# A causal convolution with matrices as taps: twelve outputs from four half-size convolutions in place of eight from three

## The chip, the cores and the metric

The kernel runs on one core of one Trainium2 chip. The core has a matrix engine (TensorE, "PE" in the profile), a vector engine (VectorE, "DVE"), a scalar engine (ScalarE, "ACT"), GpSimd ("POOL", which here only issues transfers that cast) and SyncE ("SP", which here issues stores and transposing transfers). Transfers run on 16 DMA engines. The metric is device time in microseconds (us) for one execution, as the median of several.

## The reference

```python
B, S, D, K = 8, 4096, 512, 8          # x: (8, 4096, 512) float32, kernel: (8, 512, 512) float32
out = np.zeros_like(x)
for k in range(K):
    shifted = x if k == 0 else np.concatenate([np.zeros((B, k, D)), x[:, :-k, :]], axis=1)
    out += np.matmul(shifted, kernel[k])
```

Each output row is the sum of eight products, `out[t] = x[t] W0 + x[t-1] W1 + ... + x[t-7] W7`, with 512 x 512 matrices as taps: a convolution in t whose coefficients are matrices. Done directly, one row costs eight row-by-matrix products.

## The kernel before

The 32768 rows are cut into 128 runs of 256 consecutive rows. One run belongs to each of the 128 partitions, and the kernel goes through the runs in step: "row t" below means row t of all 128 runs. Row t, transposed, is a tile of 128 partitions by 512 (four blocks of 128 channels by 128 runs), and serves as the stationary operand. A *product* is one such row times one 512 x 512 matrix, in bfloat16 with float32 sums in PSUM: four matmuls of 128x128 by 128x512.

```python
def product(bank, comp, w, start):
    for c in range(DC):                                   # DC = 4
        nc.tensor.matmul(bank, lhsT=comp[:, c * P:(c + 1) * P], rhs=w[:, c, :],
                         start=start and c == 0, stop=c == DC - 1, ...)
```

The kernel saves products in the manner of Karatsuba. Eight outputs with eight taps are made from three *half-size convolutions* of four outputs and four taps each: one with the low half of the taps, one with the high half, one with their difference (`LO`, `HI`, `MID`). Their inputs are sums of rows (`D4[t] = x[t-4] + x[t]`, and so on), made by VectorE. The same step is used twice more inside each, so that one half-size convolution, called a *node*, takes 9 products in place of 16. An iteration of the loop makes eight rows with three nodes, 27 products; there are 32 iterations.

A node uses three pairs of PSUM banks in turn for its four outputs (`p[0]` and `p[1]`, two outputs each) and a fourth pair `q` for what its parts share:

```python
def node_a1(k):                    # first product of a node; ScalarE copies it to the other bank
    product(n.q[:, 1], n.s[1][1], W[a, MID, HI], True)
    nc.scalar.copy(out=n.q[:, 0], in_=n.q[:, 1])
def node_a0(n):   product(n.q[:, 0], n.s[1][0], W[n.a, MID, LO], False)
def node_u(n):    product(n.q[:, 1], n.s[0], W[n.a, MID, MID], False)
def node_seed(n, b_):              # ScalarE starts a bank with +q or -q
    n.p[b_] = pair((2 * n.k + b_) % 3)
    ... nc.scalar.copy / nc.scalar.mul(-1.0)  (out=n.p[b_][:, 1], in_=n.q[:, 1])
def node_dts(n):  nc.scalar.copy(out=n.dts, in_=n.q[:, 0])
def node_v(n, b_): product(n.p[b_][:, 1], n.s[2][b_], W[n.a, b_, MID], False)
def node_d(n, b_):                 # VectorE starts the other bank
    tt(p[:, 0], n.dts, p[:, 1], SUB)            # or scalar_tensor_tensor for b_ == HI
def node_l(n, b_, j):              # one of the four last products
    product(n.p[b_][:, j], n.s[3][2 * b_ + j], W[n.a, b_, j], False)
def node_e(n, b_):                 # eviction of two outputs
    if n.a == MID:  nc.scalar.copy(out=ms[b_], in_=p)
    else:           tt(y, p, ms[b_], ADD if n.a == LO else SUB); store(n.i, n.a, b_, y)
```

In the loop the products of one node are interleaved with the start of the next:

```python
for k, (i, a) in enumerate(order):               # from k == 6 on
    if a == MID and more: transpose_x(i + 1, 0)
    node_l(cur, 0, LO); node_l(cur, 0, HI)
    node_a0(nxt); node_u(nxt)
    node_l(cur, 1, LO); node_e(cur, 0)
    node_seed(nxt, 0); node_seed(nxt, 1); node_dts(nxt)
    ...                                          # VectorE makes sums for later nodes
    node_v(nxt, 0); node_d(nxt, 0); node_v(nxt, 1); node_d(nxt, 1)
    ...
    node_l(cur, 1, HI); node_a1(k + 2); node_e(cur, 1)
    ...                                          # transpose_x(i + 1, 1), load_x(i + 2, ...)
```

Rows of x come in pieces of four rows: GpSimd issues a load that casts float32 in DRAM to bfloat16 in SBUF (`xin`, two buffers), and SyncE issues a transfer that transposes `xin` into `XT`, also in SBUF. The first nodes are the set-up: the weights are loaded there and their differences made, the first rows are transposed on TensorE, node 0 makes its four outputs directly with 16 products, and five nodes finish the first 16 rows. On TensorE 24 matmuls of zeros (`fill`) stand in the set-up's gaps.

Of the kernel before, what the change touches and what calls it, by code (L numbers as in the profile page):

```python
# [8 lines left out]

LO, HI, MID = 0, 1, 2


@with_exitstack
def kernel(
# [13 lines left out]
    NIT = RUN // K  # L37
    assert K == 8 and D == 512 and S % RUN == 0 and RUN % K == 0
# [13 lines left out]
    xpool = ctx.enter_context(tc.tile_pool(name="x", bufs=2))  # L52

    ctx.enter_context(tc.manual_schedule())

    W = {}
    for a in (LO, HI, MID):
        for b_ in (LO, HI, MID):
            for c_ in (LO, HI, MID):
                W[a, b_, c_] = wpool.tile([P, DC, D], bf, name=f"w{a}{b_}{c_}")  # L60

    XT = spool.tile([P, K, D], bf, name="XT")
    D4 = spool.tile([P, K, D], bf, name="D4")
    D42 = spool.tile([P, K, D], bf, name="D42")
    D421 = spool.tile([P, K, D], bf, name="D421")
    D41 = spool.tile([P, 4, D], bf, name="D41")
    D2 = spool.tile([P, 5, D], bf, name="D2")
    D21 = spool.tile([P, 4, D], bf, name="D21")
    D1 = spool.tile([P, 2, D], bf, name="D1")

    F21 = spool.tile([P, 4, D], bf, name="F21")
    F0 = spool.tile([P, D], bf, name="F0")
    A1 = spool.tile([P, 2, D], bf, name="A1")
# [4 lines left out]

    def load(out, src):
        nc.gpsimd.dma_start(out=out, in_=src)  # L80

    xin = {}

    def load_x(i, h):
        xin[i, h] = xpool.tile([P, 4, D], bf, name="xin")
        load(xin[i, h], xr[:, K * i + 4 * h:K * i + 4 * h + 4, :])

    def transpose_x(i, h):
        nc.sync.dma_start_transpose(
            out=XT[:, 4 * h:4 * h + 4, :].rearrange("p j (c m) -> p (j c) m", m=P),  # L90
            in_=xin[i, h].rearrange("p j d -> p (j d)"))


    def pairs(z):
        return z.rearrange("p (a b) d -> p a (b d)", b=2)

    def prep_m():

        tt(D1[:, 0:2], XT[:, 7::-7], XT[:, 0:2], ADD)
        tt(pairs(D2[:, 1:5]), pairs(XT)[:, 3::-3], pairs(XT)[:, 0:2], ADD)  # L100

    def prep_d27():
        tt(D2[:, 0], XT[:, 5], XT[:, 7], ADD)

    def prep_d21():
        tt(D21[:, 0:4], D2[:, 0:4], D2[:, 1:5], ADD)

    def prep_d4(h):
        a, b = (XT[:, 4:8], XT[:, 0:4]) if h == LO else (XT[:, 0:4], XT[:, 4:8])
        tt(D4[:, 4 * h:4 * h + 4], a, b, ADD)  # L110

    def prep_d41(h):
        if h == LO:
            tt(D41[:, 0:2], D4[:, 7::-7], D4[:, 0:2], ADD)
        else:
            tt(D41[:, 2:4], D4[:, 3:5], D4[:, 4:6], ADD)

    def prep_d42(h):
        if h == LO:
            tt(pairs(D42)[:, 0:2], pairs(D4)[:, 3::-3], pairs(D4)[:, 0:2], ADD)  # L120
        else:
            tt(D42[:, 4:8], D4[:, 2:6], D4[:, 4:8], ADD)

    def prep_d421(h):
        if h == LO:
            tt(D421[:, 0:4:2], D42[:, 7:0:-6], D42[:, 0:4:2], ADD)
            tt(D421[:, 1:4:2], D42[:, 0:4:2], D42[:, 1:4:2], ADD)
        else:
            tt(D421[:, 4:8], D42[:, 3:7], D42[:, 4:8], ADD)

    ppool = ctx.enter_context(tc.tile_pool(name="p", bufs=1, space=PSUM))

    def pair(k):
        return ppool.tile([P, 2, D], f32, name=f"pp{k}")

    H, HF = XT, D421.bitcast(f32).rearrange("p (t b) d -> p t (b d)", b=2)
    nc.sync.dma_start(out=HF, in_=xr[:, RUN - 4:RUN, :])
    load_x(0, 0)
    zero = spool.tile([P, D], bf, name="zero")
    nc.vector.memset(zero, 0.0)  # L145
    U1 = zero
# [5 lines left out]
    def mid(level, u, v):  # L152

        if level == 0:
            return W[MID, u, v], W[HI, u, v], W[LO, u, v]
        if level == 1:
            return W[u, MID, v], W[u, HI, v], W[u, LO, v]
        return W[u, v, MID], W[u, v, LO], W[u, v, HI]

    def mid_dve(*which):  # L160
        o, u, v = mid(*which)
        tt(o, u, v, SUB)


    def mid_neg(u, v):
        nc.scalar.mul(out=W[MID, u, v], in_=W[LO, u, v], mul=-1.0)

    def mid_acc(u, v):
        nc.gpsimd.dma_start(out=W[MID, u, v], in_=W[HI, u, v], accum_op=ADD)

    load_w(4)
    load(H[:, 1:4], xr[:, RUN - 7:RUN - 4, :])
    ident = spool.tile([P, P], bf, name="ident")
    make_identity(nc, ident)
    bank = {}

    def fill(pw):

        for h in range(2):
            nc.tensor.matmul(pw[:, h], lhsT=zero[:, 0:P], rhs=zero, start=True, stop=True)  # L180

# [7 lines left out]

    for k in range(6):  # L190
        fill(pair(k % 4))
    XF = D42


    def product(bank, comp, w, start):
        for c in range(DC):
            nc.tensor.matmul(bank, lhsT=comp[:, c * P:(c + 1) * P], rhs=w[:, c, :],  # L197
                             start=start and c == 0, stop=c == DC - 1,
                             skip_group_check=True)

    mpool = ctx.enter_context(tc.tile_pool(name="m", bufs=2))
    cpool = ctx.enter_context(tc.tile_pool(name="c", bufs=2))
    fpool = ctx.enter_context(tc.tile_pool(name="f", bufs=2))
    ypool = ctx.enter_context(tc.tile_pool(name="y", bufs=4))

    class Node:
        pass

    def streams(i, a):

        if a == MID and i == 0:
            return (F0, [D1[:, 0], D1[:, 1]], [D2[:, 1], D2[:, 3]],
                    [F21[:, j] for j in range(4)])
        if (i, a) == (1, MID):
            return (U1, [A1[:, 0], A1[:, 1]], [D21[:, 0], D21[:, 2]],
                    [F21[:, j] for j in range(4)])
        if a == MID:
            return (XT[:, 0], [D1[:, 0], D1[:, 1]], [D2[:, 1], D2[:, 3]],
                    [D21[:, j] for j in range(4)])
        o = 4 * a  # L220
        if (i, a) == (1, LO):
            return (T4[:, 0], [D41[:, 0], D41[:, 1]], [T42[:, 0], T42[:, 2]],
                    [D421[:, j] for j in range(4)])
        if (i, a) == (1, HI):
            return (D4[:, 4], [D41[:, 2], D41[:, 3]], [D42[:, 4], D42[:, 6]],
                    [D421[:, j] for j in range(4)])
        return (D4[:, o], [D41[:, 2 * a], D41[:, 2 * a + 1]], [D42[:, o], D42[:, o + 2]],
                [D421[:, o + j] for j in range(4)])

    def node_a1(k):
        n = Node()
        nodes.append(n)
        n.k, (n.i, n.a) = k, order[k]
        a = n.a  # L240
        n.s = streams(n.i, a)
        n.q = pair(3)
        product(n.q[:, 1], n.s[1][1], W[a, MID, HI], True)
        nc.scalar.copy(out=n.q[:, 0], in_=n.q[:, 1])  # L244
        n.p = {}

    def node_a0(n):
        product(n.q[:, 0], n.s[1][0], W[n.a, MID, LO], False)

    def node_u(n):  # L250
        product(n.q[:, 1], n.s[0], W[n.a, MID, MID], False)

    def node_seed(n, b_):
        n.p[b_] = pair((2 * n.k + b_) % 3)
        if b_ == LO:
            nc.scalar.copy(out=n.p[b_][:, 1], in_=n.q[:, 1])  # L256
        else:
            nc.scalar.mul(out=n.p[b_][:, 1], in_=n.q[:, 1], mul=-1.0)  # L258

    def node_dts(n):  # L260
        n.dts = cpool.tile([P, D], f32, name="dts")
        nc.scalar.copy(out=n.dts, in_=n.q[:, 0])  # L262

    def node_v(n, b_):
        product(n.p[b_][:, 1], n.s[2][b_], W[n.a, b_, MID], False)

    def node_d(n, b_):
        p = n.p[b_]
        if b_ == LO:
            tt(p[:, 0], n.dts, p[:, 1], SUB)  # L270
        else:
            nc.vector.scalar_tensor_tensor(out=p[:, 0], in0=p[:, 1], scalar=-1.0,  # L272
                                           in1=n.dts, op0=MUL, op1=SUB)

    ms = {}

    def node_l(n, b_, j):
        product(n.p[b_][:, j], n.s[3][2 * b_ + j], W[n.a, b_, j], False)

    def store(i, a, b_, y):  # L280
        t0 = K * i + 4 * a + 2 * b_
        nc.sync.dma_start(out=orr[:, t0:t0 + 2, :], in_=y)

    first = {}

    def node_y(n, b_, a):
        y = first[n.i, a, b_]
        tt(y, y, n.p[b_], ADD if a == LO else SUB)

    def node_e(n, b_):  # L290
        p = n.p[b_]
        if n.k < 4:
            pool, name = ((mpool, "ms"), (ypool, "y"), (fpool, "f"), (ypool, "y"))[n.k]
            y = pool.tile([P, 2, D], f32, name=name)
            nc.scalar.copy(out=y, in_=p)  # L295
# [40 lines left out]
    def first_run(z):  # L336

        nc.vector.memset(z[:, :, 0:D:G], 0.0)  # L338

# [308 lines left out]
```

## Time and profile before

| | |
|---|---|
| time, median of 3 | 779.59 us (779.54 to 779.87) |
| span of the profiled execution | 777.3 us |
| TensorE busy | 766.8 us, 99% |
| VectorE busy | 657.5 us, 85% |
| ScalarE busy | 284.9 us, 37% |
| DMA engines, mean busy share in the loop | about 0.8 |
| HBM read, written | 77.33 MB, 67.11 MB |

The page of the profile gives each engine's busy time and share of the span, the chain of work that ended last (followed back from the last instruction to whatever released it), and the costliest groups of instructions. A group's line reads: line of the program, engine, operation, output<-input by name, shapes and types, how often; then busy time in us and the mean of one in ns; then the idle time of the engine just before them and what ended it. "PE pp L197" in a chain is the matmul of `product`; "DVE L76" is `tt`. In a timeline each line has start, length, engine, line and operation. In a busy queue the lengths of neighbouring operations overlap a little, so the distance from start to start is what one costs.

### The profile page before, as it was taken

What the parts mean: (1) busy time and instruction counts of PE and PEld (TensorE: products, weight loads), DVE (VectorE), ACT (ScalarE), POOL (GpSimd) and SP (SyncE); (2) the same over time, 40 slices, a digit from 0 to 9 for tenths busy, and PEclk for the clock granted to TensorE, in tenths of its full rate; (3) what the DMA queues carried; (4) which work ended last, traced back from release to release, by engine and by line L of the source; (5) the groups of instructions that cost most, each with busy time, mean ns of one, the idle gap of its engine ahead of it and who ended that gap; (6) DMA issues with size and microseconds to landing.
All of it is one profiled execution on the core that took longest, in us unless ns stands there. A gap on an engine that the chain in (4) does not pass through costs nothing.

```text
span 777.3 us, 9450 instructions
## 1 busy us (share of the span) xinstructions
PE 766.8 (99%) x3584; PEld 347.3 (45%) x3584; DVE 657.5 (85%) x766; ACT 284.9 (37%) x462; POOL 42.3 (5%) x80
## 2 busy tenths in 40 slices
PE   7999999999999999999999999999999999999997
PEld 3444444444444444444444444444444444444443
DVE  4999988898888898888898888898888898888895
ACT  3553343333343333343333343333343333343332
POOL 4000000000000000000000000000000000000000
PEclk9999999999999999999999999999999999999999
DMA  9986878868786877787877878877697867687843
GB/s 199 211 125 170 226 185 178 208 159 190 164 199 163 197 172 189 164 198 169 194 171 187 164 174 190 207 162 188 163 187 176 207 158 190 165 186 179 204 133 121
DMA packets 159373, 139.42 MB, mean 179 GB/s; under 512 B 130144, under 2 KB 134240, under 8 KB 159200
## 3 DMA queue, kind: packets, MB, share of 16 engines
q1 hardware_dynamic: 145456, 99.89, 46.1%
q0 software_dynamic: 13728, 38.67, 31.6%
q8 instruction: 28, 0.46, 0.2%
q10 hardware_dynamic: 144, 0.26, 0.1%
q14 instruction: 17, 0.14, 0.1%
HBM read 77.33 MB, written 67.11 MB: 186 GB/s over the span
## 4 chain that ended last, share of the span: by engine, by line
PE 96%; DMA 2%; POOL 1%; ACT 0%; issue 0%; DVE 0%; DVEq 0%; POOLq 0%
PE pp L197 96%; DMA xin<-in_x_dram 2%; POOL w L80 0%; PE pp L186 0%; ACT y L295 0%; DVE y L76 0%; DVE pp L76 0%; POOL xin L80 0%; DVEq L647 0%; ACT pp L256 0%; ACT pp L244 0%; POOL XT L80 0%; PE pp L180 0%; POOL ident masks.py:199 0%; POOL ident masks.py:197 0%
## 5 line engine op out<-in xcount | busy, mean ns | idle before, releaser
L197 PE MATMUL pp<-w,D 128*128 128x512 bf16 x3280 | 715.5, 379 | 1.3 <-DVE w L76 0.9
L197 PEld LDWEIGHTS <-D 128*128 128x128 bf16 x3280 | 320.4, 98 | 389.8 <-issue 2.8
L76 DVE TENSOR_TENSOR D<-D 128x1024 bf16<-128x1024 bf16 (+1 forms) x252 | 228.2, 945 | 1.6 <-ACT D L353 1.6
L76 DVE TENSOR_TENSOR y<-pp,ms 128x1024 f32<-128x1024 f32 (+1 forms) x121 | 146.5, 1212 | 45.5 <-PE pp L197 45.4
L76 DVE TENSOR_TENSOR D<-XT 128x2048 bf16<-128x2048 bf16 (+2 forms) x153 | 142.1, 946 | 8.5 <-DMA XT<-xin 6.7
L244 ACT COPY pp<-pp 128x512 f32<-128x512 f32 x95 | 54.1, 570 | 256.0 <-PE pp L197 256.0
L256 ACT COPY pp<-pp 128x512 f32<-128x512 f32 x95 | 54.1, 570 | 170.6 <-PE pp L197 167.6
L76 DVE TENSOR_TENSOR pp<-dts,pp 128x512 f32<-128x512 f32 x95 | 65.5, 690 | 46.2 <-ACT dts L262 44.6
L299 ACT COPY ms<-pp 128x1024 f32<-128x1024 f32 x60 | 61.0, 1016 | 33.1 <-PE pp L197 33.1
L80 POOL DMA_DIRECT2D xin<-in_x_dram x64 | 34.2, 535 | 688.3 <-DMA XT<-xin 670.6
L272 DVE SCALAR_TENSOR_TENSOR pp<-pp,dts 128x512 f32<-128x512 f32 x95 | 65.9, 693 | 3.2
L262 ACT COPY dts<-pp 128x512 f32<-128x512 f32 x95 | 57.4, 604 | 2.0 <-PE pp L197 2.0
L258 ACT ACTIVATE pp<-pp 128x512 f32<-128x512 f32 x95 | 56.0, 589 | 1.2 <-DVE y L76 1.2
L197 PE MATMUL pp<-w,XT 128*128 128x512 bf16 x120 | 30.8, 379 | 0.0
L76 DVE TENSOR_TENSOR w<-w,w 128x2048 bf16<-128x2048 bf16 x18 | 21.6, 1219 | 0.4 <-DMA w<-in_kernel_dram 0.2
L197 PEld LDWEIGHTS <-XT 128*128 128x128 bf16 x120 | 11.7, 98 | 14.2
L180 PE MATMUL pp<-zero 128*128 128x512 bf16 x24 | 8.9, 505 | 2.4 <-DVE zero L145 1.2
L197 PE MATMUL pp<-w,w 128*128 128x512 bf16 x36 | 9.0, 379 | 1.3 <-ACT pp L244 0.7
L197 PE MATMUL pp<-w,F 128*128 128x512 bf16 x36 | 8.9, 379 | 0.0
L338 DVE MEMSET D<- 128x64 bf16 x2 | 0.2, 112 | 8.2 <-ACT D L351 7.7
L80 POOL DMA_DIRECT2D w<-in_kernel_dram x8 | 6.0, 766 | 0.8 <-DMA w<-in_kernel_dram 0.8
L197 PEld LDWEIGHTS <-w 128*128 128x128 bf16 x36 | 3.5, 97 | 5.8 <-issue 2.1
(55 smaller groups left out, 70.6 us busy)
## 6 DMA issues: line engine op xcount, KB each, us to landing
out_dram<-y SPq DMA_DIRECT2D x123, 512.0 KB, 3.5
xin<-in_x_dram POOLq DMA_DIRECT2D x64, 512.0 KB, 5.9
w<-in_kernel_dram POOLq DMA_DIRECT2D x8, 512.0 KB, 15.9
D<-in_x_dram SPq DMA_DIRECT2D x1, 1024.0 KB, 4.9
out_dram<-ms SPq DMA_DIRECT2D x2, 512.0 KB, 4.2
out_dram<-f SPq DMA_DIRECT2D x2, 512.0 KB, 3.7
XT<-xin SPq DMA_TRANSPOSE x61, 6.1
w<-w POOLq DMA_DIRECT2D x1, 512.0 KB, 9.9
```

Source lines behind the costliest of these rows:

```text
L76: nc.vector.tensor_tensor(out=o, in0=a, in1=b, op=op)
L80: nc.gpsimd.dma_start(out=out, in_=src)
L180: nc.tensor.matmul(pw[:, h], lhsT=zero[:, 0:P], rhs=zero, start=True, stop=True)
L197: nc.tensor.matmul(bank, lhsT=comp[:, c * P:(c + 1) * P], rhs=w[:, c, :], start=start and c == 0, stop=c == DC - 1, skip_group_check=True)
L244: nc.scalar.copy(out=n.q[:, 0], in_=n.q[:, 1])
L256: nc.scalar.copy(out=n.p[b_][:, 1], in_=n.q[:, 1])
L258: nc.scalar.mul(out=n.p[b_][:, 1], in_=n.q[:, 1], mul=-1.0)
L262: nc.scalar.copy(out=n.dts, in_=n.q[:, 0])
L272: nc.vector.scalar_tensor_tensor(out=p[:, 0], in0=p[:, 1], scalar=-1.0, in1=n.dts, op0=MUL, op1=SUB)
L299: nc.scalar.copy(out=ms[b_], in_=p)
L338: nc.vector.memset(z[:, :, 0:D:G], 0.0)
```

## The change

The loop makes **twelve** rows from **four** half-size convolutions. With the taps in two halves H0 and H1 of four, and rows in groups of four, three output groups need four convolutions: with the sum of the halves (`PL`), with their difference (`MI`), with `H1` and with `H0`. The first three have 9 products each. The `H0` one is a `leaf` with 11: it uses the saving step once at the outer level only, so that it has eight last products, and needs neither the corrections `node_d` nor the sums `F`. That is 38 products for twelve rows. The set-up makes the first 16 rows as before, but three of its nodes are leaves of 11 products, its last two have 9, and its order is new. After it come 20 blocks of twelve rows.

```diff
+    HEAD, STEP, R = 2 * K, 12, 20
+    NB = (RUN - HEAD) // STEP
+    ypool = ctx.enter_context(tc.tile_pool(name="y", bufs=5))
+    dpool = ctx.enter_context(tc.tile_pool(name="xd", bufs=NB * STEP // 4, space=bass.MemoryType.DRAM))
 ...
+    def zsum(o, t0, t1, n, op):          # rows t0.. and t1.. of the ring XR of 20 rows; cut at its end
 ...
+    def node_z(n):
+        if n.a == PL:   zsum(0, t - 3, t + 1, 7, ADD)
+        elif n.a == MI: zsum(4, t + 1, t - 3, 7, SUB)
+        elif n.a == H1: zsum(0, t - 7, t + 1, 7, SUB)
+        else:           zsum(7, t, t + 8, 4, SUB)
+    def node_A(n):      tt(AX[n.k % 2], n.z[:, n.o + 2:n.o + 4], n.z[:, n.o + 3:n.o + 5], ADD)
+    def node_s(n):      tt(SX[n.k % 2], n.z[:, n.o:n.o + 5], n.z[:, n.o + 2:n.o + 7], ADD)
+    def node_F(n, b_):  # not for a leaf
+        tt(F[:, 2 * b_:2 * b_ + 2], s[:, 2 * b_:2 * b_ + 2], s[:, 2 * b_ + 1:2 * b_ + 3], ADD)
 ...
+    def node_a1(n):
+        if n.leaf:
+            product(n.q[:, 1], u, W[n.a, MID, MID], True)
+            nc.scalar.mul(out=n.q[:, 0], in_=n.q[:, 1], mul=-1.0)
 ...                                      # node_seed of a leaf starts both banks of a pair from q
+    def node_l(n, b_, j):
+        if n.leaf:
+            for c_ in (LO, HI):
+                product(o, comps(n)[2][2 * b_ + j + c_], W[n.a, b_, c_], False)
 ...
+    def node_e(n, b_):
+        elif n.a == PL:
+            cc[b_] = y_tile()
+            nc.scalar.mul(out=cc[b_], in_=p, mul=0.5)
+        elif n.a == MI:
+            dd[b_] = y_tile()
+            nc.vector.scalar_tensor_tensor(out=dd[b_], in0=p, scalar=-0.5, in1=cc[b_], op0=MUL, op1=ADD)
+        elif n.a == H1:
+            y = y_tile()
+            tt(y, p, dd[b_], ADD)
+            store(t, y)
 ...
+        else:
+            tt(dd[b_], dd[b_], p, SUB)
+            store(t + 8, dd[b_])
+    def middle(n, b_):                   # g0, g1 below: the middle four rows
+        nc.vector.scalar_tensor_tensor(out=cc[b_], in0=cc[b_], scalar=2.0, in1=dd[b_], op0=MUL, op1=SUB)
+        store(n.t + 4 + 2 * b_, cc[b_])
```

The way of x changes too. A load now casts four rows from DRAM to DRAM (`xd`, a buffer for each piece), and the transposing transfer reads `xd` and writes the ring `XR`. `behind` is a copy of two elements on GpSimd that holds the loads back until a sum is made.

```diff
-        xin[i, h] = xpool.tile([P, 4, D], bf, name="xin")
-        load(xin[i, h], xr[:, K * i + 4 * h:K * i + 4 * h + 4, :])
+            xd[t] = dpool.tile([P, 4, D], bf, name="xd")
+            rows(xd[t], t, 4)
+    def behind(z):
+        nc.gpsimd.tensor_copy(out=junk, in_=z[:, 0:2])
 ...
+    SLOT = {
+        PL: "s l00 F1 a0 l01 u l11 e0 s0 s1 dt F0 z x A v0 d0 v1 d1 l10 a1 e1",
+        MI: "l00 s F1 a0 l01 u l11 e0 s0 s1 dt F0 z x A v0 d0 v1 d1 l10 a1 e1",
+        H1: "l00 s F1 a0 l01 u l11 e0 s0 s1 dt F0 z x A g0 v0 d0 v1 d1 l10 e1",
+        H0: "l00 s F1 b1 l01 a0 u l11 e0 s0 s1 dt F0 z x A g1 v0 d0 v1 d1 l10 a1 e1",
+    }
```

`SLOT` is the order of the loop's work: one line is what is issued while one node's last products run (a *slot*). `l00 l01 l10 l11`, `F1`, `e0`, `e1`, `g0`, `g1` belong to the current node; `s` (the sum S), `a0`, `u`, `s0`, `s1`, `dt`, `F0`, `v0`, `v1`, `d0`, `d1` to the next; `z` (the sum Z), `A` and `a1` to the one after (`b1` is the next node's `a1`); `x` issues transposes and loads. What a leaf lacks is skipped. In PL's slot `x` issues two transposes, in MI's one, in H1's three loads for later blocks.

## The prediction

> **What bounds the kernel now.** I read the page's first part and the chain of waits, then the chain in order of time, then VectorE's groups with shapes kept apart, then some stretches of the timeline. The page and its chain:
>
> ```profile
> span 777.3 us, 9450 instructions
> PE 766.8 (99%) x3584; PEld 347.3 (45%) x3584; DVE 657.5 (85%) x766; ACT 284.9 (37%) x462; POOL 42.3 (5%) x80
> PE 96%; DMA 2%; POOL 1%; ACT 0%; issue 0%; DVE 0%; DVEq 0%; POOLq 0%
> ```
>
> TensorE is in 96% of the chain; VectorE is next, at 85%. The granted clock is 1.000. The chain in order of time ends with one long piece:
>
> ```profile
> 45.87 726.95 PE pp L197 x3364
> 772.82 0.02 issue
> ```
>
> Columns: start, length, what. From 45.87 us to the end TensorE runs 3364 matmuls of 512 columns with no gap: 726.95/3364 = 0.2161 us each, so a product (four of them) is **P = 0.864 us**. All 3484 of these matmuls would be 752.9 us; the other **24.4 us** are about 20 in the set-up and 4.5 after the last matmul. So time follows the number of products, as long as VectorE and the transfers keep up. VectorE's groups:
>
> ```profile
> L76 DVE TENSOR_TENSOR D<-D 128x2048 bf16<-128x2048 bf16 x123 | 147.3, 1217 | 0.0
> L76 DVE TENSOR_TENSOR y<-pp,ms 128x1024 f32<-128x1024 f32 x119 | 145.2, 1221 | 45.0 <-PE pp L197 44.9
> L76 DVE TENSOR_TENSOR D<-D 128x1024 bf16<-128x1024 bf16 x127 | 81.8, 682 | 1.6 <-ACT D L353 1.6
> L272 DVE SCALAR_TENSOR_TENSOR pp<-pp,dts 128x512 f32<-128x512 f32 x95 | 65.9, 693 | 3.2
> L76 DVE TENSOR_TENSOR D<-D 128x2560 bf16<-128x2560 bf16 x1 | 1.5, 1493 | 0.0
> ```
>
> The number after the comma is the ns of one. What one costs a full queue is less: in the timeline a 1.22 us operation is followed by the next after 1.14 us, a 0.69 us one after 0.60. So I charge n/960 + 0.067 us for float32 and n/1920 + 0.067 for bf16: 1.13 (1024 float32), 0.60 (512 float32, 1024 bf16), 1.40 (2560 bf16), and, worked out in the same way, 1.93 for 3584 bf16. An operation that reads its predecessor's result loses that overlap: in the set-up a 0.68 us sum at 31.94 is followed by its reader at 32.66, so 0.12 more.
>
> The last thing to know is how closely ScalarE is coupled to TensorE:
>
> ```profile
> 31.75 1.04 PE L197 MATMUL pp<-w,D 128*128 128x512 bf16 x4
> 32.82 0.57 ACT L244 COPY pp<-pp 128x512 f32<-128x512 f32 x1 [0.93 <-PE pp L197]
> 33.44 1.02 PE L197 MATMUL pp<-w,w 128*128 128x512 bf16 x4 [0.66 <-ACT pp L244]
> ```
>
> A product started at 31.75, the copy of its bank starts 1.07 after that, and the matmul that waits for the copy starts 1.69 after it. So one other product in between (2P = 1.73 us) hides such a copy with 0.04 to spare.
>
> **What the Trainium skill says.** "TensorE: Matmul & The Clock Gate", section "Back-to-back issue gap", gives N/2.4 + 2.5 ns for one warm matmul, 215.8 ns at N = 512; the trace's 216.1 agrees (the 131 ns that it names as the sustained rate does not show here). "VectorE: DVE Perf Modes", "The perf-mode tier table": a tensor_tensor on bf16 in SBUF runs at 2x, on float32 at 1x. The trace agrees: 2048 bf16 elements and 1024 float32 ones both take 1.22. No group here is a float32 operation with both inputs in SBUF, as two of the new ones are; by that table's 1x tier I charge the same 1.13, an estimate. "Perfetto Trace Analysis", "Optimizing Scalar/DVE Operations", says that half of an operation's access overhead overlaps the next; the 0.09 us above is that. "DMA: Bandwidth & Descriptors", "Why small descriptors are slow (HBM only)": pieces of 256 B cost 11 cycles where 8 carry data, from or to HBM but not between SBUF addresses. The page counts 130144 packets under 512 B, the transposes'; the trace shows them from SBUF only.
>
> **The change part by part.**
>
> *Products.* Before: 16 for node 0 and 9 for each of 95 nodes, 871. After: 16, then three set-up nodes of 11 and two of 9, then 20 blocks of 9+9+9+11 = 38: 16 + 33 + 18 + 760 = 827, as the program's 3308 matmuls confirm. Removed: 44 products, 176 x 0.2161 = **38.0 us**. Per row the loop falls from 27/8 = 3.375 to 38/12 = 3.167 products; the set-up's 16 rows take 67 instead of 61.
>
> *VectorE in a block of 12 rows*, which TensorE does in 38P = 32.8 us: three sums Z of seven rows 5.8 and one of four 1.1; four A 2.4; four S 5.6; six F 3.6; six corrections d 3.6; six evictions e 6.8 (PL's two go to ScalarE); two middle outputs g 2.3; sums cut by the ring's end 0.1; four A that read the Z just written 0.5. Sum **31.8, 97%** of 32.8, against 85% before. This is the risk of the change.
>
> *Whether that fits in place*, in order, with t = 0 at the first matmul of H1's slot, ends in us:
>
> - H1 (TensorE 0 to 5.2): e1 of MI 0.95, S 2.35, F1 2.95 (needed by the fifth product at 3.45), e0 4.1, Z of PL 6.05, A 6.8, g0 7.9, e1 9.05. VectorE is almost 4 us late here.
> - H0 (14 products, 5.2 to 17.3): PL's first product wants A at 6.9, has it at 6.85. S 10.45, e0 11.6, F0 12.2, Z of MI 14.15, A 14.9, g1 16.0, d0 16.6, d1 17.2, e1 18.35. PL wants d0 at 17.3: 0.6 to spare.
> - PL (9 products, t = 0 anew): e1 1.1, S 2.5, F1 3.1 (needed at 3.45), F0 3.8, Z 5.7, A 6.4, d0 7.0 (needed at 7.8), d1 7.6. Its evictions are not VectorE's.
> - MI (t = 0 anew): S 1.3, F1 1.9, then VectorE waits for the second product until 2.8. Here it has caught up; lateness isn't carried to the next block.
>
> Every slack is positive, but several are 0.05 to 0.4 us. The copy that must fit in 2P occurs three times a block at a node's first product (0.02 to 0.04 spare), and PL's ScalarE eviction just ahead of a seed leaves about -0.02. I charge 0.1 to 0.3 us a block, 2 to 6 us in all, **4 us**.
>
> *Memory.* x goes to DRAM as bf16 and is transposed from there, in the same 4-row pieces: no more transfers in number, some 31 MB more written and read in HBM. A transpose is issued some 14 us before its rows are needed, and lands 6.1 us after issue at present:
>
> ```profile
> out_dram<-y SPq DMA_DIRECT2D x123, 512.0 KB, 3.5
> xin<-in_x_dram POOLq DMA_DIRECT2D x64, 512.0 KB, 5.9
> XT<-xin SPq DMA_TRANSPOSE x61, 6.1
> ```
>
> So latency is hidden. The 16 transfer engines are 79% busy in the loop (stretches of the timeline: 0.77 to 0.81); the same work in 6% less time is 83%. How much of it is transposes:
>
> ```profile
> q1 hardware_dynamic: 145456, 99.89, 46.1%
> ```
>
> This queue (packets, MB, share of the engines) carries the transposes and all 67.1 MB of stores. By bytes the transposes would be a third of it, 15%; with their small packets I put them at a quarter of the time, an estimate. At 11/8 of that cost the engines come to some 92%: full, not over.
>
> *Set-up and end.* The same loads, the same 24 fill matmuls and 76 transposes on TensorE, 20 us lost as before give or take 3; the last eviction is again two halves. No net change charged.
>
> Sum: 715 (3308 x 0.2161) + 24.4 + 4 = 743 us span; the time lies 2.3 us over the span (779.6 against 777.3): **745 us**, 4.4% less.
>
> **The rivals.**
>
> *VectorE becomes the bound.* For: 97%, and slacks of tenths of a microsecond; a 5% error in its charges makes it 33.4 a block. Against: its charges come from the same operations in this trace. It would cost 0.6 to 2 us a block: 757 to 785 us.
>
> *The y buffers.* Six buffers' worth are taken from five in a block. In the built program e1 of H1 writes the buffer that e0 of H1 stored in the same slot and waits for that store: e0 ends at 4.1, landing takes 2.1 to 7.1 us (median 3.4), so it is free at 6.3 to 11.3, and e1 is due at 7.9. At the median nothing is lost; at 5 us VectorE starts H0 1.3 late, more than the 0.6 spare there and the 0.35 in PL. If every block met that: 0.5 to 1.5 us each, 755 to 775 us.
>
> *Transposes from DRAM are slow.* If they cost twice, the queues need some 37 us a block and bind: about 820 us. For: the 256 B pieces. Against: 11/8 leaves room. One chance in twenty.
>
> *Nothing is lost and the set-up gains*, since x's first rows are asked for earlier: 737 to 741 us.
>
> **Range and chances.** The sum without stalls is 741.6 and with a set-up 3 us better 738; a slack lost in each block by one of the first two rivals brings 755 to 775. I take most of the weight near 745, a fifth between 750 and 764, and a tenth above: range 738 to 762. Within 2% begins at 764.0: faster 0.88, within 0.08, slower 0.04.
>
> **What would show it.** 3308 matmuls on the product's line at 0.216; TensorE's busy share 98 to 99%; VectorE near 90% of the whole span; few waits of TensorE on VectorE, each under 0.3 us. The y rival would show as VectorE waiting for the output's transfer at e1 of H1; the DMA rival as VectorE's Z sums waiting for the transposes, with a DMA share over 95%. I would be wrong if TensorE's waits sum to over 15 us, or if the set-up ends 5 us from where I put it (78 us).

## The result and the profile after

| | before | changed kernel | prediction |
|---|---|---|---|
| time, median | 779.57 us (779.26 to 779.87, 4 runs) | **806.6 us** (803.8 to 810.41, 4 runs) | 745 us |
| ratio | 1 | 1.0351, 95% interval 1.0322 to 1.038 | 0.956 |
| span of the profiled execution | 777.3 us | 805.4 us | 743 us |
| TensorE idle in the span | 10.5 us | 58.6 us | |

The change makes the kernel 3.5% slower. The page of the changed kernel; the four lines are the span, the busy times, the TensorE clock granted in 40 slices of the span (tenths of full speed), and the chain of work that ended last, by engine and by line:

```profile
span 805.4 us, 8887 instructions
PE 746.8 (93%) x3341; PEld 333.0 (41%) x3408; DVE 700.2 (87%) x731; ACT 248.0 (31%) x376; POOL 44.5 (6%) x98
...
PEclk9999699999999999999999999999999999999999
...
PE 51%; DMA 30%; DVE 14%; issue 2%; SPq 1%; ACT 1%; POOL 1%; DVEq 0%; another core or an unknown queue 0%; ACTq 0%; POOLq 0%
PE pp L118 51%; DMA XR<-xd 27%; DVE Z L82 6%; DMA w<-in_kernel_dram 2%; DVE S L82 2%; DVE A L82 1%; DVE y L82 1%; SPq L95 1%; DVE F L82 1%; DVE pp L82 1%; DVE pp L207 1%; DVE w L82 0%; POOL w L88 0%; DVE y L262 0%; ACT pp L188 0%
```

Before, TensorE was 96% of the chain. Now it is 51%, and 27% is one kind of transfer: `XR<-xd`, the transposes from the DRAM buffers. Mind what such a share means. It is the time in which the chain *lay on* a transpose under way, 14 us or so at a time, and most of that TensorE spent on other products. What was lost is in the list of waits (engine, line, what it waited for: us in total, times, longest):

```profile
DVE Z L82 <- DMA XR<-xd: 36.8, 16, 6.5
PE pp L118 <- DVE A L82: 31.3, 15, 4.2
PE pp L118 <- ACT pp L190: 7.5, 2, 6.8
```

VectorE's first sum of a node, `Z`, waits for transposed rows 16 times; `A` is made from `Z`, and TensorE then waits for `A` 15 times.

**Where the time went.** TensorE loads its stationary operand (PEld) once for each of the 3308 product matmuls, so these loads counted up to some moment say how far the work has come. Up to 110 us the changed kernel has done 331 of them: 110 - 331 x 0.2161 = 38.5 us lost, where before had lost 19.9 (417 done) and the prediction said 20. The remaining 2977 would take 643.3 us, and the end 4.5; they took 695.4, so **47.6 us** are lost in the loop, where the prediction charged 4. Together 715 + 38.5 + 47.6 + 4.5 = 805.6, the span. TensorE's waits after 110 us sum to 31.5 us, all but 0.2 of it for `A`. The other 16 or so, by subtraction, are matmuls that ran at a lower granted clock: after the waits of 2.6, 4.2 and 2.4 us at 161, 234 and 338 us it was 0.68, 0.71 and 0.67 over the next five to six us.

**The loop's loss**, in one block of the changed kernel's timeline (start, length, engine, line, operation; in brackets the idle time before and what ended it):

```profile
317.81 2.02 DVE L82 TENSOR_TENSOR Z<-XR 128x3584 bf16<-128x3584 bf16 x1
...
319.86 15.80 SPq L95 DMA_TRANSPOSE XR<-xd  x3
...
320.69 0.18 POOL L107 COPY junk<-A 128x2 bf16<-128x2 bf16 x1 [32.73 <-DVE A L82]
...
321.14 1.53 POOL L88 DMA_DIRECT2D xd<-in_x_dram  x3 [0.27 <-issue]
...
336.07 2.02 DVE L82 TENSOR_TENSOR Z<-XR 128x3584 bf16<-128x3584 bf16 x1 [2.44 <-DMA XR<-xd]
...
338.94 1.04 PE L118 MATMUL pp<-w,A 128*128 128x512 bf16 x4 [2.38 <-DVE A L82]
```

This is PL's slot. At 319.86 SyncE begins to issue the slot's two transposes (the row's third belongs to a later slot). 0.8 us later GpSimd's two-element copy, the work of `behind`, is released by `A`, and at 321.14 three loads of x go out. So loads and transposes share the 16 transfer engines, the rows of the second transpose come late (issued at 322.4, landed 13.5 us after), `Z` starts 2.44 us late, and TensorE loses 2.38 us. The description of the change has these three loads in H1's slot, because `x` stands in H1's line. But there `x` stands *ahead of* `A` ("z x A"), and the buffers of `A` alternate: the last write to the one that `behind` reads was the sum `A` of H1 itself, made two slots earlier, in PL's. GpSimd had nothing else to do, so the loads went out as soon as that was written.

**The set-up's loss**, in the same view:

```profile
46.32 3.96 POOL L88 DMA_DIRECT2D xd<-in_x_dram  x7
...
55.40 18.62 SPq L95 DMA_TRANSPOSE XR<-xd  x2
...
74.37 0.96 DVE L82 TENSOR_TENSOR Z<-XR 128x1536 bf16<-128x1536 bf16 x1 [6.46 <-DMA XR<-xd]
...
82.03 0.58 ACT L190 ACTIVATE pp<-pp 128x512 f32<-128x512 f32 x1 [8.13 <-DVE w L82]
...
82.66 1.87 PE L118 MATMUL pp<-w,S 128*128 128x512 bf16 x4 [6.83 <-ACT pp L190]
```

GpSimd stands until 45.8 us at an accumulating transfer, and then issues eight loads of x one after the other (46 to 52 us, the eighth at 51.80), rows 16 first; rows 36, the ninth, went out at 26.93. The transpose of rows 16 waits 13.2 us for its load, is issued at 55.40 with the later loads still under way, and lands 18.9 us after that; the one of rows 20 is issued at 70.1 and lands 6.1 us later. `Z` waits 6.46 us; two evictions that stand behind it on VectorE start at 79.59 and 80.72; ScalarE's copy into a bank waits 8.13 us for them, and TensorE 6.83 for that copy. Around the end of this stop, at 82.66, the clock is low. Two stretches (start and end, length, busy time and count of PE, PEld, DVE, ACT and POOL, then the granted clock, the transfer engines' busy share, GB/s):

```profile
80.00:90.00 10.00, 5.81 (x14) 2.03 (x14) 8.94 (x11) 1.08 (x2) 0.00 (x0) 0.53 0.53 210
90.00:100.00 10.00, 7.19 (x26) 2.78 (x25) 9.51 (x10) 2.23 (x4) 0.00 (x0) 0.84 0.55 150
```

In the first, 14 matmuls take 5.81 us of busy time, 0.42 each in place of 0.216.

### The profile page after: what moved, and what is told of

Read it like the earlier page. It is cut to its first block, busy times and chain, and to the rows that moved or that the text cites. A ratio compares the mean times of both kernels' runs of the same rounds, so it can differ in the third digit from the quotient of the medians.

```text
span 805.4 us, 8887 instructions
## 1 busy us (share of the span) xinstructions
PE 746.8 (93%) x3341; PEld 333.0 (41%) x3408; DVE 700.2 (87%) x731; ACT 248.0 (31%) x376; POOL 44.5 (6%) x98
## 3 DMA queue, kind: packets, MB, share of 16 engines
q0 software_dynamic: 13728, 38.67, 27.0%
HBM read 77.33 MB, written 98.57 MB: 218 GB/s over the span
## 4 chain that ended last, share of the span: by engine, by line
PE 51%; DMA 30%; DVE 14%; issue 2%; SPq 1%; ACT 1%; POOL 1%; DVEq 0%; another core or an unknown queue 0%; ACTq 0%; POOLq 0%
PE pp L118 51%; DMA XR<-xd 27%; DVE Z L82 6%; DMA w<-in_kernel_dram 2%; DVE S L82 2%; DVE A L82 1%; DVE y L82 1%; SPq L95 1%; DVE F L82 1%; DVE pp L82 1%; DVE pp L207 1%; DVE w L82 0%; POOL w L88 0%; DVE y L262 0%; ACT pp L188 0%
## 5 line engine op out<-in xcount | busy, mean ns | idle before, releaser
L118 PE MATMUL pp<-w,S 128*128 128x512 bf16 x1113 | 270.1, 389 | 9.7 <-ACT pp L190 6.8
L118 PE MATMUL pp<-w,F 128*128 128x512 bf16 x972 | 250.5, 382 | 2.6 <-DVE pp L82 1.5
L118 PE MATMUL pp<-w,A 128*128 128x512 bf16 x668 | 176.5, 385 | 32.8 <-DVE A L82 31.3
L82 DVE TENSOR_TENSOR Z<-XR 128x3584 bf16<-128x3584 bf16 (+2 forms) x104 | 147.8, 1436 | 39.4 <-DMA XR<-xd 36.8
L118 PEld LDWEIGHTS <-S 128*128 128x128 bf16 x1136 | 113.3, 100 | 151.0 <-issue 23.9
L118 PEld LDWEIGHTS <-F 128*128 128x128 bf16 x992 | 97.5, 98 | 121.3 <-issue 5.0
L82 DVE TENSOR_TENSOR S<-Z 128x2560 bf16<-128x2560 bf16 x80 | 118.7, 1484 | 0.0
L172 ACT COPY pp<-pp 128x512 f32<-128x512 f32 x62 | 35.3, 570 | 243.3 <-PE pp L118 237.6
L118 PE MATMUL pp<-w,Z 128*128 128x512 bf16 x380 | 96.8, 379 | 1.3 <-ACT pp L172 0.7
L82 DVE TENSOR_TENSOR F<-S 128x1024 bf16<-128x1024 bf16 x124 | 84.0, 686 | 1.7 <-PE pp L118 1.4
L247 DVE SCALAR_TENSOR_TENSOR y<-pp,y 128x1024 f32<-128x1024 f32 x40 | 48.8, 1220 | 19.9 <-PE pp L118 19.9
L262 DVE SCALAR_TENSOR_TENSOR y<-y 128x1024 f32<-128x1024 f32 x40 | 48.8, 1219 | 0.0
## 6 DMA issues: line engine op xcount, KB each, us to landing
xd<-in_x_dram POOLq DMA_DIRECT2D x60, 512.0 KB, 10.4
```

The lines of the kernel that those rows point to most:

```text
L82: nc.vector.tensor_tensor(out=o, in0=a, in1=b, op=op)
L247: nc.vector.scalar_tensor_tensor(out=dd[b_], in0=p, scalar=-0.5, in1=cc[b_], op0=MUL, op1=ADD)
L262: nc.vector.scalar_tensor_tensor(out=cc[b_], in0=cc[b_], scalar=2.0, in1=dd[b_], op0=MUL, op1=SUB)
```

## The experiments

**The theory**: loads beside the transposes. **The rivals**: VectorE, 97% full, has no room; transposes from DRAM are slow in themselves; the y buffers. All ratios are to the kernel before, with 95% intervals.

### The loads after A

```diff
-        H1: "l00 s F1 a0 l01 u l11 e0 s0 s1 dt F0 z x A g0 v0 d0 v1 d1 l10 e1",
+        H1: "l00 s F1 a0 l01 u l11 e0 s0 s1 dt F0 z A x g0 v0 d0 v1 d1 l10 e1",
```

Two words change places. The copy on GpSimd then reads the `A` made in H1's slot, and the loads go out half a block later. Nothing is removed.

> Only the order of two entries of H1's slot changes, so that the copy that holds the loads back reads the sum A of the next PL instead of H1's own and the three loads start after that block's transposes have landed. Theory 1 (the loads, issued 1.2 us after the transposes, share the engines with them and delay them): VectorE's wait for the transposes falls from 36.8 us to about 8 (the set-up's), TensorE's wait for A from 31.3 us to under 3, and with the loop's share of the clock loss (some 9 us) the time falls to 764 to 774 us. Theory 2 (a transpose that reads DRAM is slow by itself): the wait stays over 20 us and the time at 795 us or more. Theory 3 (VectorE is the bound of the loop anyway): the wait for transposes goes, waits of TensorE on VectorE take its place, time 780 to 800.

Measured: **759.29 us** (758.71 to 761.78), ratio 0.9745 [0.9726, 0.9763]: 47 us back, 5 us more than the best that was expected. The stretch of the loop, columns as above:

```profile
200.00:700.00 500.00, 499.87 (x2310) 224.53 (x2309) 482.43 (x506) 165.54 (x260) 35.24 (x56) 1.00 0.77 191
```

TensorE is busy for 499.87 of 500 us, with VectorE at 482.43: 96.5%. VectorE's small slacks hold. By the count of weight loads this kernel loses 2.0 us after 110 us, and 38.7 before: the set-up's loss is untouched.

### One and two of the three loads at the old place

```diff
                 behind(AX[cur.k % 2][:, 1])
-                for t in range(two.t + 2 * STEP, two.t + 3 * STEP, 4):
-                    load_x(t)
+                load_x(two.t + 2 * STEP)            # and a second one, + 4, in the other run
+        def more_loads():                           # a new act, after A in H1's slot
+            if two and two.t + 2 * STEP < RUN:
+                behind(AX[cur.k % 2][:, 1])
+                for t in range(two.t + 2 * STEP + 4, two.t + 3 * STEP, 4):   # or + 8
+                    load_x(t)
```

> The changed kernel with one of the three loads left at its old place beside the transposes, and two moved behind the next block's sum: a dose of the suspected cause between nought (759 us) and three (806 us). If the delay is shared bandwidth with some slack, one load (about 3.3 us of engine time) beside two transposes still lands them in time: waits for transposes about 8 us in all, time 757 to 764. If each load costs its part, a third of the loss: 771 to 777.

> The changed kernel with two of the three loads at their old place beside the transposes and one moved. None early gave 759.3 us, one 760.3, three 806.6. If the delay counts only when transposes and loads together exceed the 12.4 us between issue and need (two transposes, some 7 us of engine time, and 3.3 us a load): two loads make about 13.6, a wait of about 1 us in some blocks, time 765 to 785. If it grows evenly with the loads, 790 or so; if only the third load matters, under 763.

Measured: one early, 760.33 us (760.03 to 760.8), 0.9756 [0.9741, 0.9771]; two early, 762.33 us (760.65 to 764.37), 0.9781 [0.9762, 0.9799]. Only the third costs much. Why, the view of the transposes from 200 to 700 us shows: the operation with the min/median/max of its issue in ns, who waited for it (us, times), and the time from issue to landing. First the kernel with no load early:

```profile
DMA to landing us min/median/max: 4.3/4.9/7.9
```

One early:

```profile
DMA to landing us min/median/max: 4.4/6.1/10.2
```

Two early:

```profile
  DVE Z L82: 0.4, 1
...
DMA to landing us min/median/max: 4.2/7.1/13.2
```

Three, the changed kernel:

```profile
  DVE Z L82: 24.4, 11
...
DMA to landing us min/median/max: 4.4/7.4/17.4
```

The longest landing grows with each load, 7.9, 10.2, 13.2, 17.4, and with the third the waits for it begin. The room can be read in the run with two early. Around 304 us the view of its transposes has

```profile
L95 SPq DMA_TRANSPOSE XR<-xd x2: 2039/4820/7602, 303.3 to 305.5; - x2
...
DMA to landing us min/median/max: 7.1/9.3/11.5
```

and in its timeline the `Z` that reads them starts, without a wait, at 317.34: 11.8 us after the second was issued, 0.3 after it landed if the longer landing is that one's. So up to two loads there are paid from slack, and the third is not. Note the medians: 7.1 with two and 7.4 with three. The median does not show this at all; the longest landing does.

### The loop without its transposes

```diff
         def moves():
-            if two and two.a == H1:
-                transpose_x(two.t + 12)
-                transpose_x(two.t + 16)
-            elif two and two.a == H0:
-                transpose_x(two.t + 20)
-            elif two and two.a == PL and two.t + 2 * STEP < RUN:
+            if two and two.a == PL and two.t + 2 * STEP < RUN:
```

This kernel leaves out every transpose of the loop, so its later outputs are made from old rows. The loads stay at the changed kernel's place.

> The changed kernel without the loop's transposes: from the first block on the ring keeps its old rows, so the outputs of later rows are not computed from the right x. The loads stay where they were. Theory 1: nothing is left for VectorE to wait for; the loop runs without a gap and the time is that of the late loads, 756 to 762 us, the set-up's stall being left. If something else than the transposes held VectorE up, it stays above 780.

Measured: 760.68 us (759.9 to 761.46), 0.976 [0.974, 0.9779], the same as with late loads. The loop:

```profile
200.00:700.00 500.00, 497.35 (x2262) 223.93 (x2307) 481.91 (x505) 165.62 (x260) 24.09 (x56) 1.00 0.48 141
```

All of the loop's loss comes through the transposes, and the line gives their price: the transfer engines are 0.48 busy, against 0.77 with late loads, so 0.29 x 500 us = 145 us for 46 transposes, **3.15 us of all 16 engines each** (by the share of their queue alone, 52.0% against 24.0% of the same 500 us, 3.0). A load, by the changed kernel's page, is 2.9: the queue of the loads takes 27.0% of 805.4 us for 38.67 MB, and one load is 0.524 MB of that. Two transposes alone need 6.3 us, with one, two or three loads 9.2, 12.2 and 15.1. That is an estimate, without the stores; the longest landings lie 1 to 2.3 us above it, and the room of 11.8 falls where the waits begin.

### The set-up's loads in another order

```diff
-    load_x(36)                       # ahead of the accumulating transfer
+    load_x(16)
 ...
-    load_x(16) ... load_x(20); load_x(40) ... load_x(24); load_x(32) ... load_x(28) ... load_x(44)
+    load_x(20) ... load_x(24)
 ...
     node_A(n6)
+    behind(AX[0][:, 1]);  then load_x of 28, 32, 36
 ...
     node_A(n7)
+    behind(AX[1][:, 1]);  then load_x of 40, 44, 48
```

Once with the loop of the changed kernel, and once with late loads.

> Only the set-up's loads of x change: rows 16, 20, 24 are asked for first, and the six loads after them in two groups held back by later sums. Theory 1 (nine loads issued at once, rows 36 first, delay the first two transposes, on which VectorE waits with evictions behind it): the wait of 6.5 us at 74 us and TensorE's 6.8 us at 76 go, the granted clock stays at 1.0 between 80 and 100 us, the first block starts at 80 to 86 us in place of 102, time 786 to 792. Rival (the set-up is bound by VectorE's own work): the first block still starts after 95 us, time over 800.

> Both edits together. If they are the whole loss, the time is that of the prediction's sum, 743 to 752 us, with the clock at 0.99 or more and VectorE 93% busy. If a third cause is left (VectorE at 97% of the loop), 755 to 770, with TensorE waiting for VectorE in each block.

Measured: 804.72 us (803.73 to 808.92), 1.0332 [1.0303, 1.0361], and 758.94 us (758.55 to 760.22), 0.9737 [0.9723, 0.9752]. Both miss (the nine loads "at once" of the expectation are the eight above and the earlier rows 36): the set-up gains 2 to 3 us by the count at 110 us, and almost nothing in the time. The waits of the second kernel have no `Z` waiting for transposes, but a new entry:

```profile
DVE w L82 <- DMA out_dram<-w: 4.7, 1, 4.7
```

The first outputs are held in buffers that weight sums use again. A weight sum now waits until the store of such a buffer has landed, which takes 10.15 us in the chain of waits with the moved loads under way beside it; TensorE waits 4.9 us for that sum. The wait was moved from one transfer to another.

### Six loads put off still further

The same idea with late loads: rows 28, 32 and 36 behind the sum `A` of node 5 (57 us), rows 40, 44 and 48 at the loop's third node.

```diff
     node_A(n5)
+    behind(AX[1][:, 1]);  then load_x of 28, 32, 36
 ...
+        if k == 8:
+            behind(AX[1][:, 1]);  then load_x of 40, 44, 48
```

> As both edits together, but the set-up's later loads are placed anew: rows 28, 32, 36 follow the sum A of the last set-up node (at about 56 us, when the transfer engines are 60% busy), and 40, 44, 48 wait for the first block's H0 sum. In the run with both edits the loads of rows 28 to 36, issued at 72 us, lay beside the set-up's stores, and VectorE waited 4.7 us for a store before it could write a weight sum. Theory (the set-up's loss is again loads beside transfers that something waits for): that wait and TensorE's gap of 5 us go, the first block starts at about 86 us in place of 98, time 744 to 751 us. Rival (the set-up is limited by its own order of work, and the waits only show where): time stays at 756 to 760.

Measured: 759.32 us (758.04 to 761.9), 0.9747 [0.9727, 0.9767]: a miss. By the count the set-up gains 7.4 us (31.3 lost by 110 us), and the loop's start gives 4.4 of them back. Its waits:

```profile
DVE y L82 <- DMA out_dram<-y: 6.0, 2, 4.4
DVE Z L82 <- DMA XR<-xd: 2.6, 1, 2.6
```

Six loads are in flight between 110 and 119 us, the y stores land late, and VectorE waits 4.4 us for a y buffer: the second rival of the prediction, here at its strongest in the new loop. The changed kernel has 2.2 us of such waits in all, the one with late loads 1.7.

### The old loop with x through DRAM

Is the way through DRAM slow in itself? The kernel before, with its loads going to DRAM buffers and its transposes reading them; its first three loads stay in SBUF. First as it is, with 2 buffers, and then with one for each load, where each load is held by a copy on GpSimd that reads what the transpose before it wrote:

```diff
+    dpool = ctx.enter_context(tc.tile_pool(name="xd", bufs=2, space=bass.MemoryType.DRAM))   # bufs=61
-        xin[i, h] = xpool.tile([P, 4, D], bf, name="xin")
+        early = (i, h) in ((0, 0), (0, 1), (1, 0))
+        xin[i, h] = (xpool if early else dpool).tile([P, 4, D], bf, name="xin" if early else "xd")
+        if (i, h) not in ((0, 0), (0, 1), (1, 0), (1, 1), (2, 0)):      # the second kernel only
+            nc.gpsimd.tensor_copy(out=junk, in_=XT[:, 4 * h, 0:2])
```

In the second kernel two loads of the set-up also stand later in the program.

> The kernel before, with one part of the change alone: x goes through two buffers in DRAM in place of two in SBUF (all but the first three pieces), with the same waits. Theory 1: reading DRAM in a transpose costs little; 778 to 785 us. Theory 2 (transposes from DRAM are slow): landing of the transposes rises from 6.1 us to over 9, VectorE waits for them, 790 us or more.

> The kernel before with x through DRAM, and each load held back by a copy that reads what the transpose before it wrote, so that loads go out when the two SBUF buffers let them go out before. If reading DRAM costs a transpose nothing that matters, 778 to 784 us, with transposes landing in about 5 to 6 us. If DRAM were the cause in the run without holding (903 us), it stays above 800.

Measured: 903.12 us (902.62 to 907.53), 1.1583 [1.1563, 1.1602], and 795.8 us (794.12 to 798.17), 1.0217 [1.0193, 1.0242]. In the first, two DRAM buffers held nothing back: all loads went out between 18.7 and 187.6 us, and the transposes beside them took up to 51.3 us to land. VectorE's waits, and a stretch after the last load (columns as above):

```profile
DVE D L77 <- DMA XT<-xd: 129.7, 25, 39.4
...
240.00:700.00 460.00, 460.00 (x2132) 208.16 (x2130) 394.07 (x456) 164.63 (x276) 0.00 (x0) 1.00 0.48 136
```

This answers the question inside one run: with no load left, the same transposes from DRAM land in 4.8/5.2/6.9 us (minimum, median, maximum, from 240 us on), and TensorE has no gap in 460 us. So the 903 us are not the sign of slow transposes for which the expectation took such a time.

The second missed its expectation, 778 to 784 us. VectorE's waits and, from 200 to 700 us, the landing:

```profile
DVE D L78 <- DMA XT<-xd: 59.7, 56, 3.8
```

```profile
DMA to landing us min/median/max: 5.0/7.0/10.1
```

The kernel before waits 6.7 us in all for transposes, and theirs land in 4.9/6.1/8.3. So in this loop, where loads and transposes alternate, a transpose from DRAM lands 0.9 us later at the median, and the old loop has no room for that. The copies on GpSimd take up to 1.2 us each and delay the loads too, so not all of the 16 us need be the DRAM route's; the two were not separated. In the new loop, with late loads, a transpose from DRAM has no load beside it and lands in 4.9, sooner than the old one.

### Each load one block ahead

Late loads; in the loop the loads are for the next block, not the one after it; so fewer rows need be loaded in the set-up, and those go out in the order of their use.

```diff
-    load_x(36)
+    load_x(16); load_x(20)           # ahead of the accumulating transfer
 ...
+    load_x(24) ... load_x(28)        # after it
 ...
     node_A(n7)
+    behind(AX[1][:, 1]);  then load_x of 32, 36
 ...
-            elif two and two.a == PL and two.t + 2 * STEP < RUN:
+            elif two and two.a == PL and two.t + STEP < RUN:
                 behind(AX[cur.k % 2][:, 1])
-                for t in range(two.t + 2 * STEP, two.t + 3 * STEP, 4):
+                for t in range(two.t + STEP, two.t + 2 * STEP, 4):
                     load_x(t)
```

> Late loads in the loop, and the set-up's loads placed where nothing waits for a transfer beside them: rows 16 and 20 before the accumulating transfer that GpSimd waits 18 us for, 24 and 28 right after it, 32 and 36 behind the second block sum; rows 40 to 48 leave the set-up, because each block now loads the next block's rows in place of those of the block after. Theory (every loss so far was a load beside a transfer that something waits for): no wait of VectorE for a transfer over 1 us after 50 us, the first block starts at 84 to 90 us, time 745 to 751 us. Rival (loads one block ahead come too late, or the set-up has a floor of its own near 97 us): 755 to 765 us.

Measured: **752.23 us** (751.01 to 752.75), 0.9648 [0.9634, 0.9661]: the fastest version, 3.5% faster than the kernel before, if just over what was expected. Three stretches:

```profile
40.00:80.00 40.00, 38.12 (x174) 17.16 (x177) 35.21 (x37) 20.22 (x25) 1.98 (x3) 1.00 0.64 137
80.00:110.00 30.00, 26.57 (x120) 11.52 (x120) 29.86 (x33) 9.07 (x15) 3.15 (x3) 1.00 0.80 189
...
200.00:700.00 500.00, 497.36 (x2264) 224.80 (x2309) 481.44 (x506) 164.12 (x259) 37.41 (x60) 1.00 0.79 191
```

The clock stays at 1.00 from 40 to 110 us, where the changed kernel had 0.77 in the second of these stretches, and no `Z` waits for a transpose any more. 28.1 us are lost by 110 us, 10.4 fewer than in the changed kernel, and 2.0 after it. From 80 to 110 VectorE is busy 29.86 of 30: there it is the bound, with the last weight sums and evictions of the set-up on it. Of the 8 us that are still over the prediction's 20, about 4 fall in this stretch and 2 in each of the two before it (0 to 40 and 40 to 80 us). The run changes both the order of the set-up's loads and their number, from nine to six; which of the two counts more was not separated, and how much of VectorE's work could be moved elsewhere was not tried.

## Why the prediction was wrong

**Products: held.** 3308 product matmuls, and in the gapless loop 0.216 us each (500/2310).

**VectorE fits in place: held.** The kernel with late loads has no gap, at 96.5%; 2.0 us are lost after 110 us, where 4 were charged. The float32 operation with both inputs in SBUF, charged by the Trainium skill's "VectorE: DVE Perf Modes", "The perf-mode tier table", takes 1219 ns, like those with an input in PSUM; that charge holds. (The table's row is for tensor_tensor; the operation here is a scalar_tensor_tensor.)

**"So latency is hidden": this step failed**, and it made the sum wrong by some 44 us (47.6 lost in the loop, 4 charged). "A transpose is issued some 14 us before its rows are needed" was near (11.8 for the second of the pair in the run with two early), but "lands 6.1 us after issue" was taken from the old loop, where one transpose goes out at a time and a load is only issued when a transpose has landed. The new slot puts two transposes and three loads on the engines within 3 us, and a transpose lands up to 17.4 us after issue; TensorE's waits after 110 us sum to 31.5 us, where the prediction named 15 as a sign that it was wrong. The loads' place was read from the line of `SLOT`, not from the `A` that the copy waits for. This was in the program, and could have been seen by asking of each `behind` who wrote the buffer last.

**The engines' shares: right for the transposes, wrong for the source.** "A quarter of the time" leads to the prediction's 92% only as a quarter of all the engines' time (83% and 3/8 of 25%). For 61 transposes in 777.3 us that is 3.2 us each, and the runs show 3.0 to 3.15. But 11/8 for reading DRAM in 256 B pieces, from the skill's "DMA: Bandwidth & Descriptors", "Why small descriptors are slow (HBM only)", is not to be seen here: the queue of transposes and stores takes

```profile
q1 hardware_dynamic: 145456, 99.89, 44.5%
```

of 805.4 us, 358 us, and 46.1% of 777.3, 358 us, before. Of the "31 MB more written and read", the page shows the written part (98.57 MB, 67.11 before); its count of bytes read is 77.33 MB in every kernel, the one without the loop's transposes included, so that count does not hold their reads. The average share (0.77 with late loads, 92% predicted) was never the limit; what was put into one stretch of 12 us was.

**"No net change charged" for the set-up: this step failed too**, by 18.5 us (38.5 lost by 110 us, 20 predicted). It counted loads, fills and transposes, and found the same numbers; their order, eight loads within 6 us behind a blocked GpSimd, was not followed, nor what a stop of 6.8 us does to the clock. Loads placed anew bring 10.4 of the 18.5 us back.

**The rivals.** "VectorE becomes the bound": no, in the loop. "Transposes from DRAM are slow" gave 820 us, nearest to the measured time, and for a wrong reason: the price of a transpose is the same. Its sign, `Z` waiting for transposes, did appear, but without the share over 95% that should have come with it; that difference separates "too much to move" from "moved at the wrong moment". The y buffers: three waits, 2.2 us in all. That the copy would let the loads go too early was not among the rivals at all.

## What to carry to other kernels

A transfer's landing time belongs to the moment it runs in, not to the transfer: for each one with a deadline, list what else is issued between its issue and its deadline, and compare the sum of their engine times with that room, and the longest landing rather than the median with it. Where a transfer is held back by a small copy or a buffer, find who wrote that buffer *last*; the place of the line in the program says nothing about it. A kernel that looks short of transfer rate at a share of 0.75 may need only the order of two words changed.

## What the runs showed of the hardware that was not expected

- **A threshold, not a slope.** 0, 1, 2, 3 loads beside the pair of transposes: 759.3, 760.3, 762.3, 806.6 us, while the longest landing grows steadily (7.9, 10.2, 13.2, 17.4 us).
- **The clock after a stop.** The prediction charged nothing for it. After TensorE's 6.8 us of idle time, which ended at 82.66, the granted clock was 0.59 from 82.6 to 92.6 us and 0.83 in the ten after that. In the loop, waits of 1.4 and 1.5 us (ended at 303.47 and 126.04) leave it at 1.00; those of 2.4, 2.6 and 4.2 us are followed by 0.67 to 0.71 over five to six us, and then 1.00. Some 16 us of the loop's loss are slower matmuls, not waits.
- **The source of a transpose.** From DRAM and from SBUF its queue took the same engine time; in the old loop the landing differed, 7.0 against 6.1 us at the median, and with no load left a transpose from DRAM landed in 5.2.
- **Stores are pushed aside too.** With late loads the stores land in 7.3 us at the median, in place of 2.6; VectorE waits for one once, 1.7 us.
